# The Tanh of a split gate block written straight to its rows by ScalarE, in two of four groups, with later landings in the plan

## The chip, the cores and the metric

One NeuronCore of a Trainium2 chip runs the whole program as one launch. The metric is device time in microseconds (us), median of three runs. The core has five engines that run side by side and wait for each other through semaphores: TensorE (PE in the profile, its weight loads PEld), VectorE (DVE), ScalarE (ACT), GpSimd (POOL) and SyncE (SP), which here only issues DMA transfers. Each engine takes its instructions in the order in which they stand.

## The reference

One inference step of a two-layer trunk over 1024 prompt tokens and 8 x 4 sample tokens, 1056 columns in all, all in fp32. The first layer is a gated linear recurrence (RG-LRU). The change lies in its two gates r and i:

```python
def _rg_lru(xc, w_r, b_r, w_i, b_i, lam, h0):
    xh = xf.reshape(Bsz, T, N_BLK, BLK_W)              # 16 blocks of 96 channels
    r = sigmoid(einsum('btni,nij->btnj', xh, w_r).reshape(Bsz, T, W) + b_r)
    ig = sigmoid(einsum('btni,nij->btnj', xh, w_i).reshape(Bsz, T, W) + b_i)
    log_a = -LRU_C * softplus(-lam) * r
    a = exp(log_a)
    bterm = sqrt(-expm1(2.0 * log_a)) * (ig * xf)
    _, h = associative_scan(_lru_combine, (a, bterm), axis=1)
```

Before it stand a norm, an input projection (1024 to 2 x 1536) and a causal convolution of four taps; after it a product with silu of the gate half and an output projection with a residual. The second layer (HGRN2, a recurrence with a matrix as its state) and a last norm follow. The sigmoid is written as a Tanh of half the argument.

## The kernel before

Channels lie on partitions, tokens along the free dimension, in three chunks of 352 columns. A product in nearly full precision is three matmuls (lines 290 to 292): high part times high, high times low, low times high.

The 1536 channels of the first layer are 12 tiles of 128, in four groups g = 0 to 3 of three tiles j = 0 to 2. A group holds four blocks of 96 channels. Three of them lie whole in one tile each; the fourth is cut in three parts of 32 channels, and the part of tile j lies on partitions 32j to 32j+31 of that tile. So for each group, chunk c and gate i (0 for r, 1 for i) there are four gate products, into banks of PSUM named `hg` (four of them):

- three for the tiles j, whose Tanh (line 666) goes to `R[:, i, j]`, all 128 rows;
- a fourth for the split block (called the fo gate here). Its input is gathered first by six small DMAs from the tiles into `fo` (two parts, high and low, of three tiles; 32 rows each). Its result has 96 rows, 32 for each tile, on the very partitions that they have in the tiles. Its Tanh (line 672) goes to a buffer `td` in the tile `ST`, and three DMAs of 32 rows, `R<-ST`, copy it over the rows of `R` that the whole-tile Tanh left without meaning.

`R` has two slots, used by the chunks in turn; a slot comes free when the scans of its chunk are done. From `R` the chain goes on: exp (line 679) and a second Tanh (line 681) for each tile, a Sqrt over all three (line 689, which takes a load of another activation table ahead of it and one behind), then on VectorE the products (lines 686, 690, 692), the scan (line 706) and the product with the gate (line 716).

All this runs beside products: the input projections and convolution of the next group (lines 566 to 598) and the output projection of an earlier group (line 737 adds the residual, whose pieces SP loads and stores by DMA as `x1a` and `x1b`). SP issues nearly every DMA of the layer, the six `fo<-Z` and the three `R<-ST` of each gate among them.

The order on each engine is not written by hand. Each operation is handed to an object `Flow` with an engine, a duration, what it reads and writes; `plan` runs a list schedule over this, and the operations are emitted in the order that it found. It has a rule for when a DMA has landed, in microseconds of its own clock `t0`; `kb` is the size in kilobytes:

```python
elif kb:
    dma = max(dma, t0 + 2.6) + kb / 250.0
```

A search of 3000 random tries then improves the first 60 us of the first layer. The second layer has its own `Flow`, whose other rule for landings (`exact`) the change leaves alone. The plan only sets the order; on the chip each instruction starts when its engine and its semaphores allow.

Of the kernel before, what the change touches and what calls it, by code (L numbers as in the profile page):

```python
# [18 lines left out]
AF = mybir.ActivationFunctionType  # L19
# [31 lines left out]
CH = 352  # L51
# [9 lines left out]
class Flow:  # L61
# [67 lines left out]
    def plan(self, key, stop=None):  # L129

        n = len(self.ops)
        left = [len(o[3]) for o in self.ops]
        ready = list(self.born)
        wait = {e: [] for e in self.ENGINES}
        free = dict(self.busy)
        dma = locked = taken = 0.0
        for i in range(n):
            if not left[i]:
                wait[self.ops[i][0]].append(i)
        starts, ends, took, order = [0.0] * n, [0.0] * n, [0.0] * n, []  # L140
        for _ in range(n):
            t0, e = min((max(free[e], min(ready[i] for i in q)), e) for e, q in wait.items() if q)
            q = wait[e]
            i = min((j for j in q if ready[j] <= t0), key=lambda j: (key[j], j))
            q.remove(i)
            order.append(i)
            _, us, _, _, _, kb, _, both = self.ops[i]
            if both and not self.exact and free["POOL"] > t0:
                us = max(us, free["POOL"] - t0 + us - 0.13)
            elif both and self.exact:  # L150
                us += max(0.0, taken - t0 - 0.07)
                locked = t0 + us
            elif e == "POOL" and self.exact:
                us += max(0.0, locked - t0 - 0.035)
                taken = t0 + us
            starts[i] = t0
            free[e] = end = t0 + us
            if kb and self.exact:
                dma = max(dma + kb / 250.0, t0 + 2.4 + kb / 600.0)
                end = dma - 2.15 - kb / 250.0  # L160
            elif kb:
                dma = max(dma, t0 + 2.6) + kb / 250.0
                end = dma - 2.15 - kb / 250.0
            ends[i] = max(free[e], dma if kb else 0.0)
            took[i] = us
            if i == stop:
                break
            for j in self.after[i]:
                ready[j] = max(ready[j], free[e] if (i, j) in self.soft else end + self.lag(i, j))
                left[j] -= 1  # L170
                if not left[j]:
                    wait[self.ops[j][0]].append(j)
        last = max(t for t, o in zip(ends, self.ops) if self.until in (None, o[0]))
        return last, starts, ends, order, took
# [83 lines left out]
def tile_trunk(ctx: ExitStack, tc: tile.TileContext, xT, xN, prm, hc, w0, wg, wo0, w1, wo1, s_in,  # L258
               yT, h_out, c_out, sp_out, ss_out):
    nc = tc.nc  # L260
    V, S, G, T, Q = nc.vector, nc.scalar, nc.gpsimd, nc.tensor, nc.sync
# [12 lines left out]
    R = work.tile([128, 4, TOK], F32, tag="R", name="R")  # L274
# [13 lines left out]
    def mm3(out, w, xh, xl, first, last, more=False):  # L288
        wh, wl = w
        T.matmul(out, wh, xh, start=first, stop=False, skip_group_check=more)  # L290
        T.matmul(out, wh, xl, start=False, stop=False, skip_group_check=more)  # L291
        T.matmul(out, wl, xh, start=False, stop=last, skip_group_check=more)  # L292
# [12 lines left out]
    sm = const.tile([128, 12 * 16], F32, name="smalls")  # L305
# [39 lines left out]
    with ExitStack() as l0:  # L345
# [3 lines left out]
        def fixed(name, shape, dt=F32, pool=None):  # L349
            return (pool or pl).tile(shape, dt, tag=name, name=name)  # L350
# [7 lines left out]
        def dma(dst, src, r=(), w=(), prio=5, kb=180, q=Q, chain=None):  # L358
            fl.add("SP" if q is Q else "ACT", 0.45, lambda: q.dma_start(dst, src), r, w, prio, kb * (1.0 if r or fl.exact else 0.75),
                   line=chain)  # L360

        def act(n, emit, r, w, prio=5, more=0.0, chain=None):
            fl.add("ACT", (0.09 + 0.00088 * n if fl.exact else 0.25 + 0.0007 * n) + more, emit, r, w, prio, line=chain)
# [24 lines left out]
        t0 = fixed("t0", [128, 3, NB])  # L388
# [26 lines left out]
        def xpart(j, i, c):  # L415

            b = 6 * c + 2 * j + i
            return X[:, b * CH:(b + 1) * CH], ("X", b)
# [34 lines left out]
        def product(w, xs, step=8, more=(), bank=None):  # L453

            ps, pk = bank or next(mm)
            n = len(xs)
            for s in range(0, n, step):
                ks = range(s, min(n, s + step))

                def emit(ks=ks):  # L460
                    for k in ks:
                        mm3(ps[:, :CH], w(k)[:2], *xs[k][:2], k == 0, k == n - 1)

                fl.add("PE", (0.484 if fl.exact else 0.48) * len(ks), emit, (*(q for k in ks for q in (*xs[k][2], *w(k)[2])), *more), (pk,), 1, main=True)
            return ps, pk
# [164 lines left out]
        def lru(g):  # L630
# [16 lines left out]
            for c in range(NCH):  # L647
                s = c % 2
                R = R2[s]
# [3 lines left out]
                for j in range(3):  # L653
                    w = slice(32 * j, 32 * j + 32)
# [3 lines left out]
                for i, hb in ((0, hbr), (1, hbi)):  # L658
                    for j in range(3):
                        m = 3 * g + j  # L660
                        ps, pk = next(hg)
                        (a, ak), (b, bk) = xpart(j, 0, c), xpart(j, 1, c)
                        u = 3 * i + j
                        fl.add("PE", 0.48, lambda ps=ps, a=a, b=b, u=u: mm3(ps[:, :CH], (gh[:, u, :], gl[:, u, :]), a, b, True, True),
                               (ak, bk, ("gh", u // 4 * 4), ("gl", u // 4 * 4)), (pk,), 0)
                        act(CH, lambda ps=ps, R=R, i=i, j=j, hb=hb, m=m: S.activation(R[:, i, j], ps[:, :CH], AF.Tanh, bias=hb[:, m:m + 1],  # L666
                                                                           scale=0.5), (pk, ("sm",)), (("R", s, i, j),), 2, 0.05)
                    ps, pk = next(hg)

                    fl.add("PE", 0.48, lambda ps=ps, i=i: mm3(ps[:, :CH], (gsh[:, i, :], gsl[:, i, :]), fo[:, 0], fo[:, 1], True, True),  # L670
                           (("gs",), ("gsl",), ("fo",), *(("fo", n, j) for n in range(2) for j in range(3))), (pk,), 0)
                    act(CH, lambda ps=ps, i=i: S.activation(td[:, i], ps[:96, :CH], AF.Tanh, bias=hbd[:96, 4 * i + g:4 * i + g + 1],
                                                            scale=0.5), (pk, ("sm",)), [("ST", j, i) for j in range(3)], 2, 0.05)
                    for j in range(3):
                        w = slice(32 * j, 32 * j + 32)
                        dma(R[w, i, j], td[w, i], (("ST", j, i),), (("R", s, i, j),), 2, 45)
# [446 lines left out]
        yd = [nc.dram_tensor(f"yd_{h}", (128, TOK), F32, kind="Internal").ap() for h in range(H - 2)]  # L1123
        x1b = [nc.dram_tensor(f"x1b_{m}", (128, TOK), F32, kind="Internal").ap() for m in range(KD)]
        lru(0)
        split_y(0)
        run(project0(gate(1)))
        run(project0(conv(1)))
        gates, rest = project0(gate(2)), out(0, xT, x1a)
        run(islice(gates, 6))  # L1130
        lru(1)
        run(gates)
        run(project0(conv(2)))
        lru(2)
        run(rest)
        split_y(1)
# [19 lines left out]
    with ExitStack() as l1:  # L1156
# [644 lines left out]
        def yparts(c):  # L1801
            return [(yh[k][:, chunk(c)], yl[k][:, chunk(c)], (("yh", k, c), ("yl", k, c))) for k in range(K1)]
# [22 lines left out]
        for n, (m, c) in enumerate([(m, c) for c in range(NCH) for m in range(2)] + [(m, c) for m in range(2, KD) for c in range(NCH)]):  # L1825
# [11 lines left out]
            ps, pk = product(ws2[m], yparts(c), 8 if m > 1 else 1)  # L1837
# [90 lines left out]
        for (a, n), RM, SM in zip(OUT, RMS, SMS):  # L1928
# [4 lines left out]
            for m in range(KD):  # L1933
# [9 lines left out]
                ps, pk = next(mm)  # L1943
# [96 lines left out]
```

## Time and profile before

| what | us |
|---|---|
| median of 3 runs | 1031.67 (1030.27 to 1032.05) |
| the profiled execution | 1029.75 |
| its span in the trace | 1027.9 |
| TensorE busy | 1013.2, 99% of the span |
| VectorE, ScalarE, GpSimd busy | 777.6, 610.3, 494.6 |
| Tanh to `ST` (line 672) | 24 of 548 ns each |

The span begins with the first instruction and ends with the last; the execution's own time is 1.85 us longer. "Busy" for TensorE is modelled from start times, since matmuls overlap, so the count of matmuls that start in a stretch of fixed length tells more than its busy share. Times within the trace are us from the span's start. The first layer takes up about 0 to 510; its groups 2 and 3 have their gates between about 220 and 390. In a view of waits, a row names the waiting engine and line, what it waited for, the total, how many times, and the longest.

### The profile page before, as it was taken

To read this page: it belongs to the slowest core of one execution; us is meant where nothing else is said; L and a number is where in the kernel's file an instruction comes from. 1 tells how busy PE (TensorE), PEld (TensorE's weight loads), DVE (VectorE), ACT (ScalarE), POOL (GpSimd) and SP (SyncE) were. 2 spreads that over 40 slices of the span, in tenths; PEclk is the share of its full clock that TensorE was granted. 3 is DMA by queue.
4 is the path that set the end of the run, shared out by engine and by line. 5 is a ranking of instruction groups with operands and counts; after the bars stand their busy time and mean duration, and the time that the engine had idled before them with its cause. 6 is when DMAs were issued, how large, how long until landed. Compare 5 with 4: busy or idle time off the path is not lost.

```text
span 1027.9 us, 25651 instructions
## 1 busy us (share of the span) xinstructions
PE 1013.2 (99%) x9981; PEld 993.5 (97%) x9981; DVE 777.6 (76%) x1538; ACT 610.3 (59%) x1405; POOL 494.6 (48%) x579
## 2 busy tenths in 40 slices
PE   9999999999999999999999999999999999999997
PEld 9999999999999999999999999999999999999986
DVE  6899986798689688557798787787777777885537
ACT  7678656876765666434566474646565564752324
POOL 2435453454247254744235655564646464641544
PEclk9999999999999999999999999999999999999999
DMA  9611111214652478622113142423333333666204
GB/s 283 204 53 43 51 61 61 79 55 134 202 186 71 145 224 270 201 72 77 62 32 125 46 141 89 127 87 126 106 119 111 106 125 98 212 197 208 87 1 170
DMA packets 84442, 124.60 MB, mean 121 GB/s; under 512 B 11296, under 2 KB 61728, under 8 KB 84320
## 3 DMA queue, kind: packets, MB, share of 16 engines
q1 hardware_dynamic: 75104, 107.13, 33.6%
q10 hardware_dynamic: 9216, 15.84, 4.8%
q8 instruction: 78, 1.28, 0.5%
q14 instruction: 44, 0.36, 0.1%
HBM read 82.55 MB, written 33.87 MB: 113 GB/s over the span
## 4 chain that ended last, share of the span: by engine, by line
PE 86%; DVE 5%; ACT 3%; issue 2%; DMA 2%; POOL 1%; SPq 0%; POOLq 0%; DVEq 0%; ACTq 0%
PE mm L290 24%; PE mm L292 24%; PE mm L291 24%; PE hg L1281 2%; DVE k L594 2%; DMA R<-ST 1%; PE hg L1470 1%; PE hg L291 1%; PE hg L290 1%; PE hg L1513 1%; PE hg L292 1%; PE hg L1515 1%; PE hg L902 1%; PE hg L1538 1%; DVE R L706 1%
## 5 line engine op out<-in xcount | busy, mean ns | idle before, releaser
L290 PE MATMUL mm<-xh,whi 128*128 128x352 f32 (+1 forms) x1111 | 343.0, 309 | 0.3 <-DVE xo L737 0.3
L291 PE MATMUL mm<-xl,whi 128*128 128x352 f32 (+1 forms) x1111 | 340.8, 307 | 1.0 <-POOL xl L374 1.0
L292 PE MATMUL mm<-xh,wlo 128*128 128x352 f32 (+1 forms) x1111 | 341.5, 307 | 0.0
L374 POOL TENSOR_TENSOR wlo<-wraw,whi 128x256 fp32r<-128x256 f32 (+3 forms) x190 | 194.4, 1040 | 180.4 <-ACT whi L436 81.4
L291 PEld LDWEIGHTS mm<-xl,whi 128*128 128x128 f32 x1111 | 209.1, 188 | 1.5 <-POOL xl L374 1.2
L290 PEld LDWEIGHTS mm<-xh,whi 128*128 128x128 f32 x1111 | 208.8, 188 | 1.1 <-issue 0.6
L292 PEld LDWEIGHTS mm<-xh,wlo 128*128 128x128 f32 x1111 | 208.8, 188 | 0.2 <-DVE wlo L374 0.2
L290 PE MATMUL mm<-Z,whi 128*128 128x264 f32 (+1 forms) x507 | 152.2, 300 | 0.0
L291 PE MATMUL mm<-Z,whi 128*128 128x264 f32 (+1 forms) x507 | 150.5, 297 | 0.0
L292 PE MATMUL mm<-Z,wlo 128*128 128x264 f32 (+1 forms) x507 | 150.5, 297 | 0.0
L290 PEld LDWEIGHTS mm<-Z,whi 128*128 128x128 f32 x507 | 95.3, 188 | 2.7 <-ACT xh L1798 1.5
L594 DVE SCALAR_TENSOR_TENSOR k<-xb,prm_sb,k 128x352 f32<-128x352 f32 (+2 forms) x144 | 91.8, 646 | 7.4 <-ACT k L591 4.5
L291 PEld LDWEIGHTS mm<-Z,whi 128*128 128x128 f32 x507 | 95.5, 188 | 0.3
L292 PEld LDWEIGHTS mm<-Z,wlo 128*128 128x128 f32 x507 | 95.5, 188 | 0.2 <-POOL wlo L762 0.2
L374 POOL TENSOR_TENSOR wlo<-R,whi 128x256 fp32r<-128x256 f32 x74 | 59.4, 822 | 47.0 <-ACT whi L1640 40.6
L685 POOL TENSOR_TENSOR k<-Z 128x352 f32<-128x352 f32 x36 | 44.4, 1242 | 74.0 <-DVE R L686 64.4
L436 ACT CAST whi<-wraw 128x512 fp32r<-128x512 f32 (+2 forms) x75 | 41.2, 568 | 28.5 <-PE mm L291 11.6
L1710 DVE TENSOR_TENSOR k<-mm,k 128x264 f32<-128x264 f32 x58 | 24.5, 425 | 40.5 <-PE mm L292 33.7
L1640 ACT CAST whi<-wraw 128x512 fp32r<-128x512 f32 x61 | 37.6, 616 | 24.5 <-PE mm L291 24.4
L1707 ACT COPY k<-mm 128x264 f32<-128x264 f32 x84 | 31.7, 377 | 32.7 <-PE mm L292 29.8
L666 ACT ACTIVATE R<-hg,smalls 128x352 f32<-128x352 f32 x72 | 38.1, 550 | 14.7 <-DVE R L706 8.4
L290 PE MATMUL mm<-xh,Z 128*128 128x352 f32 x140 | 45.7, 327 | 0.0
(455 smaller groups left out, 2337.5 us busy)
## 6 DMA issues: line engine op xcount, KB each, us to landing
wraw<-in_w_dram SPq DMA_DIRECT2D x50, 256.0 KB, 3.3
wraw<-in_w_dram ACTq DMA_DIRECT2D x39, 256.0 KB, 3.2
wraw<-in_wo_dram SPq DMA_DIRECT2D x34, 192.0 KB, 2.7
R<-in_w_dram ACTq DMA_DIRECT2D x18, 256.0 KB, 2.8
si<-in_s_in_dram SPq DMA_DIRECT2D x8, 512.0 KB, 6.2
vt<-sg SPq DMA_DIRECT2D x8, 512.0 KB, 4.0
sg<-vt SPq DMA_DIRECT2D x32, 128.0 KB, 3.4
kt<-xo SPq DMA_DIRECT2D x8, 512.0 KB, 2.6
```

Of the source, the lines that this page charges most:

```text
L290: T.matmul(out, wh, xh, start=first, stop=False, skip_group_check=more)
L291: T.matmul(out, wh, xl, start=False, stop=False, skip_group_check=more)
L292: T.matmul(out, wl, xh, start=False, stop=last, skip_group_check=more)
L374: emit = lambda: e.tensor_tensor(b, x, a.bitcast(F32), op=ALU.subtract)
L436: act(m, lambda: S.copy(hi[:, :m], raw[:, :m]), rk, (hk,), prio, chain=chains[0])
L594: dve(u, lambda src=src, dst=dst, sh=sh, k=k: V.scalar_tensor_tensor(dst, sh(src, k), pc("cw", 12 * k + m), dst, op0=ALU.mult, op1=ALU.add ...
L666: act(CH, lambda ps=ps, R=R, i=i, j=j, hb=hb, m=m: S.activation(R[:, i, j], ps[:, :CH], AF.Tanh, bias=hb[:, m:m + 1], scale=0.5), (pk, ("s ...
L685: pool(CH, lambda x=x, a=a, b=b: G.tensor_tensor(x, a.bitcast(F32), b.bitcast(F32), op=ALU.add), (ak, bk), (xk,), 3)
L1281: T.matmul(ps[32 * j:32 * j + 32, n * w:n * w + w], B[:, o:o + 32], q(slice(o, o + 32)), start=True, stop=True, tile_position=(0, 32 * j))
L1640: act(512, lambda: S.copy(hi, raw), (rk,), (hk,), 2)
L1707: act(QT, lambda: S.copy(o[0], z[0]), (z[1],), (o[1],), 0)
L1710: dve(QT, lambda: V.tensor_tensor(o[0], z[0], u[0], op=ALU.add), (z[1], u[1]), (o[1],), 0)
```

## The change

In the third and fourth group (g = 2 and 3) the fo gate's Tanh no longer goes to `td` and from there by DMA. Three Tanh instructions of 32 rows and 352 columns read the bank and write `R[w, i, j]` directly, and the `continue` leaves the three DMAs out. Groups 0 and 1 keep the buffer and the DMAs. In the plan's rule for landings, a DMA that starts between 60 and 385 us of the plan's clock counts as landed 0.8 us later than before. Lines behind the new block move down by six (679 becomes 685, 681 becomes 687, 689 becomes 695).

```diff
             elif kb:
-                dma = max(dma, t0 + 2.6) + kb / 250.0
+                dma = max(dma, t0 + (3.4 if 60.0 < t0 < 385.0 else 2.6)) + kb / 250.0
                 end = dma - 2.15 - kb / 250.0
...
                     fl.add("PE", 0.48, lambda ps=ps, i=i: mm3(ps[:, :CH], (gsh[:, i, :], gsl[:, i, :]), fo[:, 0], fo[:, 1], True, True),
                            (("gs",), ("gsl",), ("fo",), *(("fo", n, j) for n in range(2) for j in range(3))), (pk,), 0)
+                    if g in (2, 3):
+                        for j in range(3):
+                            w = slice(32 * j, 32 * j + 32)
+                            act(CH, lambda ps=ps, R=R, w=w, i=i, j=j: S.activation(R[w, i, j], ps[w, :CH], AF.Tanh, bias=hbd[w, 4 * i + g:4 * i + g + 1],
+                                                                                   scale=0.5), (pk, ("sm",)), (("R", s, i, j),), 2, 0.05)
+                        continue
                     act(CH, lambda ps=ps, i=i: S.activation(td[:, i], ps[:96, :CH], AF.Tanh, bias=hbd[:96, 4 * i + g:4 * i + g + 1],
                                                             scale=0.5), (pk, ("sm",)), [("ST", j, i) for j in range(3)], 2, 0.05)
```

Both edits change the plan's input, so the order moves on every engine through the first layer. On TensorE the last row that differs lies at the norm of the last chunk of the first layer's output; from there on, the whole second layer included, its rows stand as before.

The first place is SP's queue in group 2, ahead of the gather of the last chunk's `fo` (the second batch of six of this group; `x1a` is the residual's storage, `xo`, `k` and `xb` its landing buffers, `wraw` weights). Before:

```order
L359 DMA R<-ST 32x352
L359 DMA x1a<-xb_140 128x352
L359 DMA x1a<-k 128x352
L359 DMA k<-in_xT_dram 128x352
L359 DMA R<-ST 32x352 x2
L359 DMA k<-in_xT_dram 128x352
L359 DMA x1a<-xb_138 128x352
L359 DMA R<-ST 32x352
L359 DMA xb_139<-in_xT_dram 128x352
L359 DMA wraw<-in_w_dram 128x512
L359 DMA fo<-Z 32x352 x6
```

With the change:

```order
L359 DMA x1a<-k 128x352
L359 DMA wraw<-in_w_dram 128x512
L359 DMA xo<-in_xT_dram 128x352
L359 DMA x1a<-k 128x352
L359 DMA xo<-in_xT_dram 128x352
L359 DMA wraw<-in_w_dram 128x512
L359 DMA x1a<-k 128x352
L359 DMA k<-in_xT_dram 128x352
L359 DMA fo<-Z 32x352 x6
```

The copies to `R` are gone. Between the chunk's gather and the one ahead of it stand 20 transfers before and 17 now.

The second place is ScalarE in group 3, around the exp of the second chunk. Before, with the Tanh to `ST`, the casts of weights (436), the exps (679) and the whole-tile Tanhs (666) that empty gate banks behind them:

```order
L672 ACTIVATE ST<-hg,smalls 96x352
L436 CAST whi<-wraw 128x384 x2
L666 ACTIVATE R<-hg,smalls 128x352
L672 ACTIVATE ST<-hg,smalls 96x352
L679 ACTIVATE a<-R,smalls 128x352
L681 ACTIVATE R<-R,smalls 128x352
L679 ACTIVATE a<-R,smalls 128x352
L681 ACTIVATE R<-R,smalls 128x352
L666 ACTIVATE R<-hg,smalls 128x352 x2
```

With the change (675 is the new Tanh):

```order
L675 ACTIVATE R<-hg,smalls 32x352
L666 ACTIVATE R<-hg,smalls 128x352
L675 ACTIVATE R<-hg,smalls 32x352 x2
L685 ACTIVATE a<-R,smalls 128x352
L666 ACTIVATE R<-hg,smalls 128x352
L687 ACTIVATE R<-R,smalls 128x352
L685 ACTIVATE a<-R,smalls 128x352
L666 ACTIVATE R<-hg,smalls 128x352
L675 ACTIVATE R<-hg,smalls 32x352 x3
L687 ACTIVATE R<-R,smalls 128x352
L685 ACTIVATE a<-R,smalls 128x352
L687 ACTIVATE R<-R,smalls 128x352
```

The exp now stands behind Tanhs of its own engine, and Tanhs that empty gate banks stand between the exps, where before two stood behind two exps.

## The prediction

> **What bounds the kernel now.** I read the page's busy line first, then the table of stretches, then the waits of TensorE, and from there the timelines of the engines that it waited for.
>
> ```profile
> PE 1013.2 (99%) x9981; PEld 993.5 (97%) x9981; DVE 777.6 (76%) x1538; ACT 610.3 (59%) x1405; POOL 494.6 (48%) x579
> 100.00:150.00 50.00, 50.00 (x313) 50.00 (x313) 45.34 (x80) 29.58 (x63) 23.34 (x24) 1.00 0.18 53
> 250.00:300.00 50.00, 48.23 (x296) 47.16 (x295) 39.05 (x66) 34.37 (x58) 19.50 (x19) 1.00 0.73 221
> 300.00:350.00 50.00, 49.49 (x308) 49.20 (x308) 42.16 (x72) 30.70 (x69) 25.57 (x32) 1.00 0.27 79
> 350.00:400.00 50.00, 48.13 (x292) 46.61 (x291) 35.41 (x55) 39.47 (x65) 22.07 (x16) 1.00 0.76 235
> ```
>
> TensorE sets the time; only its lost time can be won. The stretches count its matmuls: 313 in 50 us where nothing disturbs it, 0.16 us apiece. The three stretches that hold groups 2 and 3 have 17, 5 and 21 fewer: 43 matmuls, 6.9 us. The clock was granted in full (1.00), so these are waits. More than 6.9 us is not to be had from these groups. Finer stretches place the loss (64 matmuls is a full one):
>
> ```profile
> 100.00:110.00 10.00, 10.00 (x64) 10.00 (x64) 10.00 (x13) 3.88 (x10) 7.23 (x6) 1.00 0.17 58
> 270.00:280.00 10.00, 8.52 (x51) 8.04 (x51) 7.73 (x12) 6.88 (x9) 1.56 (x1) 1.00 0.70 212
> 280.00:290.00 10.00, 9.71 (x59) 9.12 (x58) 8.62 (x12) 4.20 (x8) 8.02 (x7) 1.00 0.87 259
> 330.00:340.00 10.00, 9.49 (x60) 9.20 (x59) 9.75 (x21) 5.97 (x15) 4.47 (x9) 1.00 0.22 62
> 350.00:360.00 10.00, 9.79 (x58) 8.99 (x57) 2.88 (x6) 9.56 (x14) 2.07 (x2) 1.00 0.61 179
> 360.00:370.00 10.00, 8.79 (x55) 8.44 (x53) 8.07 (x12) 5.70 (x12) 4.93 (x3) 1.00 0.77 235
> 370.00:380.00 10.00, 9.55 (x57) 9.28 (x58) 7.19 (x11) 8.37 (x13) 6.22 (x5) 1.00 0.60 171
> ```
>
> Call the loss at 270 to 280 A (13 matmuls, 2.1 us), at 280 to 290 B (5, 0.8), at 330 to 340 C (4, 0.65), at 350 to 360 D (6, 1.0), at 360 to 380 E (16, 2.6). What ended each is in TensorE's waits from 255 to 400 us:
>
> ```profile
> PE hg L290 <- ACT R L666: 1.5, 1, 1.5
> PE hg L290 <- DMA fo<-Z: 1.2, 1, 1.2
> PE hg L291 <- DVE Z L598: 0.5, 1, 0.5
> PE mm L290 <- DVE xo L737: 0.3, 1, 0.3
> ```
>
> The first is E: a gate product found no free bank, since ScalarE had not run the Tanh that empties one. The second is A: the gather of `fo` was late. C and B wait for VectorE.
>
> **Part 1: the copies leave the chain (E and D).** ScalarE's timeline shows why the bank was late:
>
> ```profile
> 350.33 0.68 ACT L679 ACTIVATE a<-R,smalls 128x352 f32<-128x352 f32 x1 [2.92 <-DMA R<-ST]
> 362.51 0.55 ACT L672 ACTIVATE ST<-hg,smalls 96x352 f32<-96x352 f32 x1
> 367.08 0.69 ACT L679 ACTIVATE a<-R,smalls 128x352 f32<-128x352 f32 x1 [4.02 <-DMA R<-ST]
> 369.68 0.98 ACT L666 ACTIVATE R<-hg,smalls 128x352 f32<-128x352 f32 x2
> ACT a L679 <- DMA R<-ST: 9.2, 5, 4.0
> ```
>
> The exp needs the 32 rows that the DMA brings. After the Tanh to `ST` ended at 363.1 ScalarE stood idle for 4.0 us, and behind the waiting exp stood the two Tanhs that empty gate banks; they ran at 369.68, and TensorE's gate product followed. D is the same with 2.9 us. The changed order has only ScalarE's own Tanhs ahead of the exp, so no landing is waited for. These two places go: 1.0 + 2.6 = 3.6 us.
>
> Here the Trainium skill speaks against the change: "DMA: Bandwidth & Descriptors", Rules for kernel authors, has a DMA issued early and its semaphore waited for late, so that the fixed cost overlaps with compute; by that rule the copies would be free and removing them worth 0. The 9.2 us in the last row disagree for this place.
>
> **Part 2: SP's queue (A).** It was full from 249 to 293 us:
>
> ```profile
> L359 SPq DMA_DIRECT2D R<-ST x13: 507/513/582, 249.8 to 292.7; - x13
> 263.57 0.51 SPq L359 DMA_DIRECT2D R<-ST  x1
> 265.76 1.15 SPq L359 DMA_DIRECT2D R<-ST  x2
> 268.11 0.51 SPq L359 DMA_DIRECT2D R<-ST  x1
> 269.82 3.68 SPq L359 DMA_DIRECT2D fo<-Z  x6
> 272.73 0.32 PE L292 MATMUL mm<-Z,wlo 128*128 128x352 f32 x1
> 274.25 0.40 PE L290 MATMUL hg<-fo,gsh 128*128 128x352 f32 x1 [1.20 <-DMA fo<-Z]
> ```
>
> The fo gate started 4.4 us after the first of the six issues (274.25 - 269.82). Ahead of them four copies took 0.51 + 1.15 + 0.51 us with about 0.05 us between issues: 2.3 us. Without them the gather starts at 267.5 and the gate could start at 271.9, ahead of the 272.9 at which TensorE got there. The wait of A goes: 2.1 us. In the order with the change 54 matmuls (8.7 us) stand between the last fo gate of the chunk before and this one, as before, and SP has 17 transfers in between in place of 20; in group 3, between the last two gathers, 14 in place of 23.
>
> **Part 3: what ScalarE pays.** Twelve Tanhs of 96 rows become 36 of 32. No row shows that form. The nearest:
>
> ```profile
> L672 ACT ACTIVATE ST<-hg,smalls 96x352 f32<-96x352 f32 x24 | 13.2, 548 | 1.0 <-PE hg L292 0.5 <-DMA R<-ST 0.3
> L666 ACT ACTIVATE R<-hg,smalls 128x352 f32<-128x352 f32 x72 | 38.1, 550 | 14.7 <-DVE R L706 8.4 <-POOL ST L711 2.4 <-PE hg L292 2.0
> L1345 ACT COPY attn<-attnd 32x256 f32<-32x256 f32 x32 | 12.9, 403 | 0.8 <-DVE attnd L1285 0.5
> L1350 ACT COPY attn<-hg 32x128 f32<-32x128 f32 x16 | 4.0, 249 | 3.0 <-PE hg L1360 2.4 <-DVE attn L1350 0.3
> ```
>
> 96 and 128 rows cost the same (548 and 550 ns), so height does not count; the copies of 32 rows grow by 154 ns for 128 columns, which puts 352 columns at 0.52 us. Bounds 0.52 and 0.55; I take 0.55, the row of the same function. The 24 added Tanhs are 13.2 us of ScalarE. Over 250 to 400 us it was busy for 34.4 + 30.7 + 39.5 = 104.6 of 150 us and waited 9.2 us for these copies, so 13.2 - 9.2 = 4.0 us come out of 36 us that it stood idle for other reasons. That hides the cost on average. Where gates stand close it may not: a bank of an fo gate comes free after 3 x 0.55 us in place of one, 1.1 us later, and each of the twelve could hold up the next gate by that. Bounds: nothing, and 4.0 us, all that ScalarE carries beyond what it no longer waits for. Only four of the twelve stand where gates came too late in the trace (D and E); I take 1.2 us, about one such delay.
>
> Best Practices in "Trainium Kernel Development and Optimization" of the Trainium skill says to tile to 128 partitions; three pieces of 32 break it, and by it this edit is a loss on ScalarE. [...]
>
> **Part 4: a new wait on ScalarE.** The Tanh to `ST` needed no slot of `R`. The new one writes `R`, so it waits until the scans of two chunks earlier are done, with every bank behind it. Whole-tile Tanhs wait so already, 4.8 us in all:
>
> ```profile
> ACT R L666 <- DVE R L706: 4.8, 2, 4.0
> ```
>
> The fo Tanhs stand in the new order behind a whole-tile Tanh of the same slot, which has had that wait by then. Bounds 0 and 4.0 us (the longest); I take 0.
>
> **Part 5: later landings, and the rest of the order.** In the stretch 245 to 392 us the DMAs of the copies' buffer landed after:
>
> ```profile
> DMA to landing us min/median/max: 1.8/3.2/5.2
> ```
>
> The plan's 2.6 + 44 KB x 4 ns was 2.8 us, now 3.6: nearer this median, so gates that need a gather are placed later. C and B (1.45 us) wait for VectorE, whose work this does not change: I leave them where they are, though the first gate of C moved nine matmuls (1.4 us) later. Groups 0 and 1 are re-planned too, with their copies kept. The stretch from 60 to 260 us shows no loss (the x313 row stands for it), so nothing can be won and something lost. The bound above is the density of groups 2 and 3, 6.9 us in 150, over these 200 us: 9.2 us. That density came from copies and gathers that were later than planned, and the new plan has them later, so I take 0.2 us, near the zero of the row itself.
>
> **The sum**, against the profiled execution (1029.75 us, of which 1027.9 us span): A 2.1 + D 1.0 + E 2.6 = 5.7 us less; 1.2 + 0.2 = 1.4 us more; net 4.3 us less, 1025.45. The median of the runs shown is 1.9 us above that execution, so for a median: 1031.67 - 4.3 = **1027.4 us**. Behind the first layer TensorE's order is unchanged, and what is won there arrives at the end.
>
> **Rivals.** *The time moves to other waits.* With the copies gone the chain's next late link is VectorE: exps done sooner meet scans still queued behind the convolution, and the next gates wait for slots of `R` as they waited for copies. For it: VectorE was 97% busy from 330 to 340. Against it: in D and E VectorE had time (2.88 of 10 us at 350 to 360). Then only A is won, 2.1 us, and the 1.4 us are paid: 1031.0.
>
> *ScalarE becomes the bound (slower).* From 350 to 360 it was busy for 9.56 of 10 us while TensorE lost time. If the gates keep standing where ScalarE is that full, every fo gate holds the next one up by its 1.1 us: 12 x 1.1 = 13.2 us against 5.7 won, 1039.2. An fo gate pays once ScalarE has less than 1.1 us to spare between it and the gate that takes its bank next; from the sixth that pays (5.7 / 1.1 = 5.2) the change is a loss. Against it: 36 us of idle in the three stretches.
>
> *The new plan costs more in groups 0 and 1 than it wins.* Three new waits of the size of A (2.1 us) would turn the gain into 2.0 us of loss: 1033.7. For it: VectorE is busier there (45.34 of 50 us in the x313 row) than later. Against it: the row of zero loss, under a plan that counted on earlier landings. *The edit does nothing that the plan would not do*: the gates moved by the landings alone avoid A and E, and the direct Tanh adds only its cost; the time would be the forecast's, and only a run with one edit tells.
>
> **Numbers.** A difference under 0.2%, 2.1 us, cannot be told from none here. Forecast 0.66 (4.3 us; from all of 6.9 us down to 2.5), other waits 0.18 (1031.0), ScalarE or groups 0 and 1 slower 0.12, between them 0.04. Faster: 0.66 and a third of the second, 0.72. Slower 0.10, the rest 0.18 the same. The range runs from 1031.67 - 6.9 = 1024.8 to 1032.0, past the second case; the forecast's own is 1024.8 to 1029.2.
>
> **What would show it.** Right: from 250 to 300 and 350 to 400 us the count of matmuls is at least 305 each; no row in which ScalarE or VectorE waits for `R<-ST` after 250 us; the new Tanhs at 0.52 to 0.56 us; ScalarE's busy time up by 13 us; SP with idle time ahead of the gathers. Wrong: TensorE's waits name Tanh lines 666 or 675 with 3 us or more, or waits appear between 60 and 250 us; or the Tanh of 32 rows costs well over 0.55 us.

## The result, and the profile after

| | before | after |
|---|---|---|
| median of 4 runs, us | 1030.97 (1030.16 to 1032.05) | 1024.81 (1023.94 to 1025.56) |
| the profiled execution, us | 1029.75 | 1025.03 |
| its span, us | 1027.9 | 1023.3 |

The ratio is 0.9939, with a 95% interval from 0.9922 to 0.9957: 6.2 us less, 4.4 to 8.0. A second comparison on another chip gave 0.9952 [0.9940, 0.9965], 4.9 us. The pair of profiled executions differs by 4.7 us. So the change makes the kernel faster, as forecast. The first comparison has 6.2 us where the sum had 4.3, with a median at the fast end of the forecast's own range (1024.8); the second has 4.9 us (3.6 to 6.2).

The page's busy line of the changed kernel:

```profile
PE 1012.5 (99%) x9981; PEld 994.0 (97%) x9981; DVE 782.6 (76%) x1538; ACT 623.6 (61%) x1429; POOL 494.2 (48%) x579
```

ScalarE is busy 13.3 us longer (623.6 - 610.3), nearly the 13.2 us of part 3, and TensorE is still 99% busy. The three stretches of groups 2 and 3, with the columns as in the prediction:

```profile
250.00:300.00 50.00, 48.77 (x303) 48.53 (x302) 41.02 (x73) 45.74 (x77) 18.88 (x20) 1.00 0.71 226
300.00:350.00 50.00, 50.00 (x313) 50.00 (x312) 42.44 (x71) 31.48 (x71) 24.52 (x32) 1.00 0.27 84
350.00:400.00 50.00, 50.00 (x311) 49.77 (x310) 39.31 (x61) 47.15 (x82) 23.59 (x19) 1.00 0.79 243
```

303, 313 and 311 matmuls stand where 296, 308 and 292 stood: 12 are missing from three times 313 in place of 43. At 0.16 us each that is 1.9 us lost in place of 6.9, a gain of 5.0 us. ScalarE's columns went from 34.4, 30.7 and 39.5 us to 45.7, 31.5 and 47.2: two of the three stretches are nearly full now.

Where E stood, ScalarE's timeline now reads:

```profile
363.45 1.12 ACT L675 ACTIVATE R<-hg,smalls 32x352 f32<-32x352 f32 x2
364.60 0.68 ACT L685 ACTIVATE a<-R,smalls 128x352 f32<-128x352 f32 x1
365.31 0.55 ACT L666 ACTIVATE R<-hg,smalls 128x352 f32<-128x352 f32 x1
365.76 0.67 ACT L687 ACTIVATE R<-R,smalls 128x352 f32<-128x352 f32 x1
366.33 0.67 ACT L685 ACTIVATE a<-R,smalls 128x352 f32<-128x352 f32 x1
```

Line 685 is the exp (679 before). It starts when the direct Tanh ends, with no wait, and the Tanh 666 that empties a bank follows at once. What TensorE still waits for between 200 and 420 us is one row:

```profile
PE hg L290 <- ACT R L666: 1.2, 1, 1.2
```

This wait did not exist before. It lies at 250 us, in the first gates of group 2, and the timeline shows its history:

```profile
248.65 0.49 ACT L597 CAST Z<-k 128x352 fp32r<-128x352 f32 x1 [2.86 <-DVE k L594]
249.04 0.51 ACT L436 CAST whi<-wraw 128x384 fp32r<-128x384 f32 x1
249.57 1.28 ACT L666 ACT_TABLE_LOAD   x1
250.87 0.55 ACT L666 ACTIVATE R<-hg,smalls 128x352 f32<-128x352 f32 x1
251.47 0.43 PE L290 MATMUL hg<-Z,gh 128*128 128x352 f32 x1 [1.23 <-ACT R L666]
```

ScalarE waited 2.86 us for VectorE's convolution (line 594) before a cast. A cast of weights and a load of the table (1.28 us) stood between that cast and the Tanh that empties the first bank. No direct Tanh has run by then; the first one starts at 254.3. The lost time here, taken from the starts of the matmuls around it, is 1.5 us.

### The profile page after: what moved, and what is told of

It reads as the page before. It is cut to its first block, busy times and chain, and to the rows that moved or that the text cites. A ratio compares the mean times of both kernels' runs of the same rounds, so it can differ in the third digit from the quotient of the medians.

```text
span 1023.3 us, 25600 instructions
## 1 busy us (share of the span) xinstructions
PE 1012.5 (99%) x9981; PEld 994.0 (97%) x9981; DVE 782.6 (76%) x1538; ACT 623.6 (61%) x1429; POOL 494.2 (48%) x579
## 3 DMA queue, kind: packets, MB, share of 16 engines
q8 instruction: 78, 1.28, 0.5%
## 4 chain that ended last, share of the span: by engine, by line
PE 93%; DVE 2%; ACT 1%; DMA 1%; POOL 1%; issue 1%; SPq 0%; POOLq 0%; DVEq 0%; ACTq 0%
PE mm L290 26%; PE mm L292 26%; PE mm L291 26%; PE hg L1287 2%; PE hg L290 2%; PE hg L291 2%; PE hg L292 2%; PE hg L1476 1%; PE hg L1519 1%; PE hg L1521 1%; DMA sg<-in_xN_dram 1%; PE hg L1544 1%; PE hg L1374 0%; DMA sg<-in_xT_dram 0%; POOL sg L1919 0%
## 5 line engine op out<-in xcount | busy, mean ns | idle before, releaser
L374 POOL TENSOR_TENSOR wlo<-wraw,whi 128x256 fp32r<-128x256 f32 (+3 forms) x190 | 191.4, 1024 | 184.5 <-ACT whi L436 90.9
L594 DVE SCALAR_TENSOR_TENSOR k<-xb,prm_sb,k 128x352 f32<-128x352 f32 (+2 forms) x144 | 89.7, 633 | 10.7 <-ACT k L591 5.5
L290 PE MATMUL mm<-xh,Z 128*128 128x352 f32 x140 | 45.8, 327 | 0.0
L292 PE MATMUL mm<-xh,Z 128*128 128x352 f32 x140 | 45.2, 323 | 0.0
```

What stands on the lines that cost most here:

```text
L374: emit = lambda: e.tensor_tensor(b, x, a.bitcast(F32), op=ALU.subtract)
L594: dve(u, lambda src=src, dst=dst, sh=sh, k=k: V.scalar_tensor_tensor(dst, sh(src, k), pc("cw", 12 * k + m), dst, op0=ALU.mult, op1=ALU.add ...
```

## The experiments

Eleven runs of ten kernels were made, each of five executions or more, beside the kernel before on the same chip. The last two columns are what the trace says: matmuls started in 250 to 300, 300 to 350 and 350 to 400 us, and how many of 3 x 313 are missing, times 0.16 us.

| kernel | median, us | ratio to before, interval | matmuls | lost, us |
|---|---|---|---|---|
| before, four sets | 1029.9 to 1031.2 | | 296, 308, 292 | 6.9 |
| changed, again | 1025.00 | 0.9952 [0.9940, 0.9965] | 305, 313, 313 | 1.3 |
| direct Tanh alone | 1023.18 | 0.9926 [0.9913, 0.9939] | 313, 312, 313 | 0.2 |
| the same, again | 1023.46 | 0.9933 [0.9920, 0.9945] | 313, 313, 312 | 0.2 |
| later landings alone | 1030.93 | 0.9997 [0.9985, 1.0009] | 306, 313, 286 | 5.4 |
| copies in the new order | 1051.49 | 1.0198 [1.0182, 1.0215] | 254, 288, 268 | 20.6 |
| idle copies added | 1028.22 | 0.9973 [0.9964, 0.9982] | 297, 313, 298 | 5.0 |
| each direct Tanh twice | 1033.97 | 1.0039 [1.0027, 1.0052] | 291, 295, 286 | 10.7 |
| one of three twice | 1026.51 | 0.9958 [0.9945, 0.9971] | 305, 311, 304 | 3.0 |
| direct in group 2 only | 1027.09 | 0.9960 [0.9945, 0.9975] | 313, 313, 276 | 5.9 |
| direct in group 3 only | 1026.18 | 0.9955 [0.9943, 0.9967] | 297, 313, 313 | 2.6 |
| direct in all groups | 1024.10 | 0.9944 [0.9930, 0.9957] | 312, 313, 313 | 0.2 |

6.9 less the last column follows the measured gain (by the ratio) to 1.2 us in all rows but two (the copies in the new order, and group 2 only), of which the text says more.

### Which edit does it

The theory was that the direct Tanh brings the gain, by its two effects: no landing ahead of the exp, no copies in SP's queue. The rival was that the later landings in the plan would do the same by moving the gates. Each edit was made alone. The direct Tanh alone:

```diff
-                dma = max(dma, t0 + (3.4 if 60.0 < t0 < 385.0 else 2.6)) + kb / 250.0
+                dma = max(dma, t0 + 2.6) + kb / 250.0
```

> The direct Tanh in groups 2 and 3 alone, the plan's landings left at 2.6 us. The order on TensorE then stands as before up to the gates of group 2 (about 245 us). Theory (copies on ScalarE's chain and in SP's queue cost the time): the waits A, D and E are gone without any help of the later landings, TensorE makes at least 305 matmuls in 250 to 300 and in 350 to 400 us, and the time is 5 to 7 us below before, 1024 to 1026. Rival (the later landings moved the gates out of the way): the time stays within 2 us of before, 1029 to 1033.

Measured: 1023.18 us, by the ratio 7.6 us under the kernel before. Its stretches lose nothing:

```profile
250.00:300.00 50.00, 50.00 (x313) 50.00 (x312) 39.25 (x69) 44.84 (x75) 17.20 (x17) 1.00 0.69 211
300.00:350.00 50.00, 50.00 (x312) 50.00 (x312) 41.48 (x69) 33.37 (x75) 25.22 (x33) 1.00 0.36 105
350.00:400.00 50.00, 50.00 (x313) 50.00 (x312) 39.51 (x57) 45.65 (x79) 26.39 (x20) 1.00 0.72 223
```

The later landings alone:

```diff
-                    if g in (2, 3):
+                    if False:
```

> The later landings alone, with the Tanh to the buffer and the copies kept in all groups. Theory: the copies still take SP's queue and still hold up the exp, so ScalarE keeps waiting for them by more than 4 us in all after 250 us; the time is within 2.5 us of before, 1028.5 to 1033. Rival: the plan now reckons with the copies, waits A, D and E go, and the time is 1024 to 1026.

Measured: 1030.93 us, by the ratio 0.3 us under the kernel before, which cannot be told from none. The exp waits for the copies again, as the waits of ScalarE and TensorE from 250 to 420 us show:

```profile
ACT a L685 <- DMA R<-ST: 7.9, 5, 3.7
PE hg L290 <- ACT a L685: 1.7, 1, 1.7
PE hg L290 <- ACT R L666: 0.8, 1, 0.8
```

The table of stretches shows that the rival holds for one part: with the landings alone the losses A, B and C shrink (306 and 313 matmuls in the first two stretches in place of 296 and 308), while the third loses more (286 in place of 292). A later landing in the plan moves a gate behind its gather; it does not take the exp out of the chain. The gain of the change is therefore the direct Tanh's.

The direct Tanh alone was 1.6 us better than the whole change, on different chips. Both were run again on one chip.

> The changed kernel once more, beside the direct Tanh without the later landings, on one chip. If the later landings cost nothing, both give the same time, between 1023 and 1025 us. If they cost the new wait of ScalarE and TensorE at 250 us (1.5 us) and the 1.2 us more at the start, this one is 1.5 to 2.7 us above the other.

> Direct Tanh in groups 2 and 3, the plan's landings left at 2.6. If the first run's 1.6 us below the change was the chip and not the kernel, it falls within 0.5 us of the changed kernel here. If it was the order, it is again 1.5 us or more below, with no lost matmul between 60 and 420 us.

Measured: 1025.00 and 1023.46 us, 1.5 us apart as in the first runs. The wait at 250 us stands in both traces of the change (1.5 and 1.2 us lost) and in that of the landings alone (1.0 us), and in neither trace of the direct Tanh alone. So the landings cost about what this wait costs, and the direct Tanh alone is the best version that was found. The first 60 us, the other half of what was expected here, do not separate the two: 357 and 353 matmuls start there in the two traces of the change, 357 and 352 in the two of the direct Tanh alone (362 in the trace of the kernel before). They vary from execution to execution.

### Does each loss have its place, or is it a lucky order

A new plan moves hundreds of instructions. If the gain came from that alone, it would not be bound to a group. The direct Tanh was made in one group at a time, with the landings of the kernel before.

```diff
-                    if g in (2, 3):
+                    if g == 2:
```

> Direct Tanh in group 2 alone, landings left at 2.6. By parts 1 and 2 each loss has its place: the copies in SP's queue at 263 to 268 us (A) are those of group 2, the exps that wait (D, E) stand in group 3. Then A goes (2.1 us, with B 2.9) and D and E stay (3.6): 1.8 to 2.9 us under the kernel before, with waits of exp for R<-ST and lost matmuls only after 340 us. Rival that the direct Tanh only gives the plan another order, which happens to be good: no place is bound to a group, and either all is won (6 us) or nothing.

```diff
-                    if g in (2, 3):
+                    if g == 3:
```

> Direct Tanh in group 3 alone, landings left at 2.6. By the same parts: D and E go (3.6 us, with C 4.2), A and B stay (2.9): 3.6 to 4.2 us under the kernel before, lost matmuls between 260 and 300 us and none from 340 to 400. Rival of the lucky order: as above, all or nothing, or losses in other places.

Measured: 1027.09 us for group 2 alone (4.1 us less, 2.6 to 5.7) and 1026.18 for group 3 alone (4.6 us less, 3.4 to 5.9). The places are those that were named. With group 2 alone, the stretch that holds A and B is whole and the loss is in group 3:

```profile
270.00:280.00 10.00, 10.00 (x64) 10.00 (x63) 8.39 (x15) 8.58 (x13) 4.86 (x4) 1.00 0.76 251
280.00:290.00 10.00, 10.00 (x64) 10.00 (x63) 10.00 (x13) 7.28 (x13) 5.78 (x5) 1.00 0.93 300
350.00:400.00 50.00, 47.51 (x276) 47.01 (x276) 34.77 (x58) 37.56 (x64) 21.54 (x16) 0.93 0.75 233
```

With group 3 alone it is the other way round:

```profile
270.00:280.00 10.00, 9.38 (x56) 8.56 (x54) 7.23 (x12) 8.74 (x12) 1.85 (x2) 1.00 0.68 205
280.00:290.00 10.00, 10.00 (x61) 9.51 (x60) 9.52 (x12) 3.18 (x8) 9.29 (x7) 1.00 0.93 289
350.00:400.00 50.00, 50.00 (x313) 50.00 (x312) 39.87 (x64) 45.64 (x79) 23.59 (x19) 1.00 0.81 252
```

The rival of the lucky order falls as the main cause. Both medians are somewhat past what was expected (2.9 and 4.2 us at most), with the expected ends inside the intervals. C (0.65 us), counted only in the second, is gone in both; so much a new order does by itself. With group 2 alone, the gain in the table (6.9 - 5.9 = 1.0 us) falls short of the measured 4.1: the profiled execution was the longest of six, 1029.0 us of 1024.68 to 1029.0, and what happened in it at 366 us is told in the last section. The loss there is in the place that was named, but not by the wait that was named: TensorE waited for a gather (1.8 us), not for a bank. Ahead of that gather SP issued three copies in one piece (1.78 us from 360.08), so it is part 2's mechanism in group 3.

### What the copies cost by themselves: the chain, and the queue

To have the queue's share alone, an idle transfer was added behind each direct Tanh, at its place in SP's queue and with the copy's shape. Its data goes to a scratch array that nobody reads; the order is otherwise that of the change.

```diff
+                            def piece(ps=ps, R=R, w=w, i=i, j=j, c=c):
+                                S.activation(R[w, i, j], ps[w, :CH], AF.Tanh, bias=hbd[w, 4 * i + g:4 * i + g + 1], scale=0.5)
+                                Q.dma_start(nc.dram_tensor(f"dum_{g}_{c}_{i}_{j}", (32, CH), F32, kind="Internal").ap(), td[w, i])
```

> The changed kernel and its order, with 36 transfers of 32 x 352 from the unused buffer to memory that nobody reads, issued on SP where the direct Tanhs stand. Nobody waits for them; they only take SP's queue as the copies did. Theory by its second part: the gathers of fo are late again by up to 2 us at one to three places, 1 to 4 us more than the changed kernel, 1026 to 1029. Rival (SP's queue was never the point, only the exp's wait was): within 1 us of the changed kernel, 1024 to 1026.

Measured: 1028.22 us, 3.4 and 3.2 us above the two medians of the change (by the centres of the ratios 3.5 and 2.2); the lost time in the three stretches rises from 1.9 to 5.0 us. Three places of lost time are new. At 377 us a gather is late again, as SP's timeline in group 3 shows:

```profile
371.14 1.15 SPq L359 DMA_DIRECT2D fo<-Z  x2
372.34 0.57 SPq L678 DMA_DIRECT2D dum<-ST  x1
372.95 0.51 SPq L359 DMA_DIRECT2D fo<-Z  x1
...
375.30 1.14 SPq L359 DMA_DIRECT2D fo<-Z  x2
377.41 0.40 PE L290 MATMUL hg<-fo,gsh 128*128 128x352 f32 x1 [0.82 <-DMA fo<-Z]
```

In the changed kernel the same six stood in one piece, and their gate product waited for nothing:

```profile
369.37 3.70 SPq L359 DMA_DIRECT2D fo<-Z  x6
374.93 0.32 PE L290 MATMUL hg<-fo,gsh 128*128 128x352 f32 x1
```

The issue of the last of the six ended at 373.1 there and at 376.4 here: three idle transfers stand between the six and hold SP for 0.58 us each. At 357 us TensorE waited 0.6 us for VectorE's addition to the residual, which had itself waited 2.8 us for the piece that SP loads. The third place, a fo gate at 285.9 us, is put down to a cast on ScalarE (0.6 us). So 36 transfers that nobody waits for cost 3.4 us. Part 2's mechanism is shown by the gather at 377 us. How much of the rest is SP's time and how much the added traffic was not separated, and the size is that of these 36 places, not of A, where the copies of the kernel before stood elsewhere.

The other experiment put the copies back in full, at the direct Tanhs' places in the new order: one Tanh of 96 rows to `td` in place of the first of three, and a copy in place of each.

```diff
-                            act(CH, lambda ...: S.activation(R[w, i, j], ps[w, :CH], AF.Tanh, ...), (pk, ("sm",)), (("R", s, i, j),), 2, 0.05)
+                            def piece(ps=ps, R=R, w=w, i=i, j=j, seen=seen):
+                                if not seen:
+                                    seen.append(1)
+                                    S.activation(td[:, i], ps[:96, :CH], AF.Tanh, bias=hbd[:96, 4 * i + g:4 * i + g + 1], scale=0.5)
+                                Q.dma_start(R[w, i, j], td[w, i])
...
+                            act(CH, piece, (pk, ("sm",)), (("R", s, i, j),), 2, 0.05)
```

> The changed kernel's order on all engines, but in groups 2 and 3 the first of each three Tanhs writes 96 rows to the buffer, and the copies are issued on SP where the three Tanhs stood. Theory: waits for R<-ST are back on ScalarE (more than 5 us) and the gates behind them stall TensorE; 1029 to 1036. Rival (the order is what pays): 1024 to 1027, as the changed kernel.

Measured: 1051.49 us, 20 us above the kernel before, and far above what was expected. The waits of ScalarE and TensorE name it:

```profile
ACT a L692 <- DMA R<-ST: 40.2, 12, 7.4
PE hg L290 <- ACT R L666: 8.0, 6, 2.6
PE mm L290 <- ACT whi L436: 3.1, 1, 3.1
```

The exp waited twelve times, 40.2 us in all, where before it waited five times, 9.2. The loss goes on past the three stretches: from 400 to 450 us 266 matmuls started, 47 or 7.5 us fewer, so 28 us are lost in all, 21 more than before. This order was planned with the rows of `R` ready when ScalarE's own Tanh ends, so it puts the exp right behind. It says nothing on what the copies cost in the order that was planned for them; it says that the direct Tanh and the order found for it belong together, and that what stands behind a waiting exp on ScalarE (bank Tanhs, casts of weights) reaches TensorE in this order.

The Trainium skill, "DMA: Bandwidth & Descriptors", Rules for kernel authors, has a DMA that is issued early and waited for late overlap its fixed cost with compute. The runs agree for groups 0 and 1, which keep their copies while TensorE loses nothing from 60 to 249 us. Here they do not: the copies cost TensorE time both through the exp and, with nobody waiting for them, through the queue.

### What ScalarE still has to spare

Part 3 charged the 24 added Tanhs 1.2 us, and one rival let every fo gate pay 1.1. Both were tried by adding more of the same, in the order of the change. Every direct Tanh twice:

```diff
+                            def piece(ps=ps, R=R, w=w, i=i, j=j):
+                                for _ in range(2):
+                                    S.activation(R[w, i, j], ps[w, :CH], AF.Tanh, bias=hbd[w, 4 * i + g:4 * i + g + 1], scale=0.5)
```

> The changed kernel in its own order, each of the 36 direct Tanhs issued twice on the same rows: 36 x 0.55 = 19.8 us more of ScalarE, the result the same. The Tanhs stand in 250 to 300 and 350 to 400 us, 18 in each, 9.9 us more in each; ScalarE had 4.3 and 2.8 us idle there. Theory that idle time covers them on average (the backlog is worked off where TensorE does not wait for it): the time of the change, at most 2 us above. Rival that ScalarE is at its bound in these two stretches: 5.6 + 7.1 = 12.7 us above the change, about 1037, with TensorE waiting for lines 666 and 675. I expect a part of the second, 1028 to 1035.

Measured: 1033.97 us, 9.0 us above the change on the same chip and 4.0 above the kernel before. ScalarE is full in two of the stretches (47.66 and 48.32 of 50 us), and TensorE's waits from 240 to 420 us, behind them, name it:

```profile
250.00:300.00 50.00, 47.57 (x291) 46.42 (x290) 35.88 (x63) 47.66 (x83) 18.80 (x20) 1.00 0.73 225
350.00:400.00 50.00, 48.05 (x286) 45.58 (x285) 33.60 (x55) 48.32 (x81) 18.80 (x17) 1.00 0.72 222
```

```profile
PE hg L290 <- ACT R L666: 3.1, 4, 1.4
PE hg L290 <- ACT Z L597: 1.6, 1, 1.6
PE hg L290 <- ACT R L678: 0.8, 2, 0.4
```

(Line 678 is the direct Tanh of this kernel.) Then only the last of the three pieces twice:

```diff
-                                for _ in range(2):
+                                for _ in range(2 if j == 2 else 1):
```

> The changed kernel in its own order, the last of the three direct Tanhs of each fo gate issued twice: 12 x 0.55 = 6.6 us more of ScalarE, 3.3 in each of the two stretches that have 4.3 and 2.8 us idle. If idle time covers what ScalarE pays until it is full, this costs 0 to 1 us: 1025 to 1026. If every added Tanh costs the same from the first on, as 36 of them cost 9.0 us, it costs 12 x 0.25 = 3.0 us: 1028.

Measured: 1026.51 us, 1.5 us above the change by the medians, 0.6 to 2.0 by the centres of the ratios. That is between the two expectations. The trace has new lost time of 1.1 us at 347 to 352 and 0.8 at 363, in addition to the wait at 250. Together the runs give a curve: the 24 Tanhs that the change adds cost TensorE nothing that any trace shows (the direct Tanh alone loses nothing in its three stretches), 12 more cost about 1.5 us (0.13 each), and the 24 after these another 7.5 (0.31 each). One rival is left: the plan knew of the first 24 and not of the others, which stand in an order made without them. So the runs show that this order has no room for more; that an order planned for 12 more would have none either is not shown.

### Would more of the same help

```diff
-                    if g in (2, 3):
+                    if True:
```

with the landings of the kernel before.

> Direct Tanh in all four groups, landings at 2.6. TensorE lost nothing from 60 to 250 us with the copies of groups 0 and 1 in place, so by the theory that only lost TensorE time can be won there is nothing to gain: 1023 us, as with groups 2 and 3 alone. Rival that the copies cost something in every group: another 3 to 6 us less, under 1020. Rival that ScalarE's further 13.2 us fall where it is full (35 of 50 us busy before): up to some 3 us more, with TensorE waiting for a Tanh before 250 us.

Measured: 1024.10 us, against 1023.46 for groups 2 and 3 alone on the same chip: no further gain. Its three stretches are whole (312, 313, 313), as are those of the version beside it. Where TensorE lost nothing (60 to 250 us), taking copies away wins nothing.

## Where the prediction was right, and which step failed

**What bounds the kernel**: right. The lost matmuls of TensorE, at 0.16 us each, follow the time through the runs, from 0.2 us lost at 1023 us to 10.7 at 1034.

**Part 1 (D and E)**: right. No row of the changed kernel has ScalarE or VectorE waiting for `R<-ST` after 250 us. With the direct Tanh in group 3 alone the stretch 350 to 400 is whole; with the landings alone, or in group 2 alone, it is not. But a wait of the exp does not always reach TensorE: with the direct Tanh in group 3 alone the exps still waited five times for copies, 6.6 us in all, and TensorE waited for none of ScalarE's Tanhs. VectorE's wait for the copies was the larger one, as its waits in the kernel before from 250 to 420 us show:

```profile
DVE R L686 <- DMA R<-ST: 15.1, 7, 3.9
```

In the changed kernel the same product (line 692) waits 2.9 us for the direct Tanh in its place.

**Part 2 (A)**: right in mechanism. The idle copies bring a late gather back. The sign "SP with idle time ahead of the gathers" was too much: for 3.7 us ahead of the second gather of group 2 SP still issues almost back to back, and the pause before that is a wait of SP's own (1.6 us, for GpSimd). What the gather gained is the distance to its gate, 8.5 us from the first issue in place of 4.4, and the gate waits for nothing:

```profile
276.90 3.68 SPq L359 DMA_DIRECT2D fo<-Z  x6
285.44 0.32 PE L290 MATMUL hg<-fo,gsh 128*128 128x352 f32 x1
```

**Part 3**: the price was right, the charge was not. The page's row of the new form:

```profile
L675 ACT ACTIVATE R<-hg,smalls 32x352 f32<-32x352 f32 x36 | 19.6, 544 | 1.0 <-PE hg L292 0.4
```

544 ns for 32 rows against 548 for 96 and 550 for 128: height does not count, as was taken. "Best Practices" in "Trainium Kernel Development and Optimization" of the Trainium skill says to tile to 128 partitions. By this row three short pieces do cost three full prices, and the time came down nevertheless. The 1.2 us charged to TensorE were not paid: the direct Tanh alone loses nothing. **Part 4** (no new wait for a slot of `R`): right; the 1.0 us of idle ahead of line 675 names no scan. (The 4.8 us "in all" of its row are those between 255 and 400 us; the row of line 666 in part 3 has 14.7 us for the whole program.)

**Part 5** failed in both its terms. It left C and B, 1.45 us, where they were, because VectorE's work does not change: they are gone. B goes wherever A goes (change, landings alone, group 2 alone) and shrinks from 5 missing matmuls to 3 where A stays (group 3 alone), with no wait of TensorE left there. Whether B followed from A or moved with the plan, no run separates. C is in none of the plans made with either edit. A wait for an engine whose work does not change still moves with the plan. The other term, 0.2 us for what the new plan loses from 60 to 260 us, was to be 1.5: the re-plan with later landings put a cast that waits 2.9 us for VectorE, a cast of weights and a table load ahead of the first gate's Tanh at 250 us, at the seam of group 1 and group 2.

**The sum.** Won in the three stretches were A to E, 6.9 us in place of 5.7; paid were 1.9 (in the trace of the second run of the change 1.3) in place of 1.4. That is 5.0 us against the 4.3 forecast. Outside of them five fewer matmuls start in the first 60 us (357 in place of 362, 0.8 us lost); the pair of profiled executions differs by 4.7 us, so 0.5 us more are won in other places. For the profiled execution the forecast was 1025.45 us and the result 1025.03. That it came so close is in part luck: the terms of parts 3 and 5 were each off by more than 1 us, and partly cancel.

**The step to the median** is the one that failed by most. The prediction added the 1.9 us by which the median of before, 1031.67, lay above the profiled execution, as if this distance belonged to the program. In the changed kernel the median lies 0.2 us below its profiled execution (1024.81 and 1025.03), in the second run of the same kernel 0.7 above (1025.00 and 1024.29). So the distance is the spread of single executions and does not carry over; it makes 2.1 of the 2.6 us between the forecast of 1027.4 and the measured median, and the other 0.4 is the profiled execution's. The second comparison, 4.9 us, is nearer to the forecast's 4.3 than the first.

Why executions of one kernel differ stays open. Those of the kernel before range from 1028.96 to 1035.17 us in one set of 21, those of the change from 1023.94 to 1025.84 in nine, and only one execution of each set has a trace. The granted clock bears on it: of 41 executions of the kernel before, run beside the experiments, the 22 with a mean clock of 0.998 or more average 1030.1 us, the 19 with less 1031.7. No trace of a long execution of that kernel shows where its clock fell.

**The signs.** No wait of ScalarE or VectorE for `R<-ST`, the price of the Tanh and ScalarE's 13 us came as said. The count of at least 305 matmuls was missed in the first stretch (303; 305 in the second run) by the wait at 250 us, which also lies at the edge of the sign of being wrong, "waits appear between 60 and 250 us".

**The rivals.** *Other waits*: one appeared (250 us), of 1.5 us. TensorE waited for ScalarE there, which had waited for VectorE as the rival has it, but for the convolution and not for a slot of `R`. *ScalarE becomes the bound*: it did not, but 36 Tanhs more in the same order come to 4.0 us above the kernel before. *Groups 0 and 1*: no wait of TensorE between 60 and 249 us in either trace of the change. *The plan alone would do it*: A, B and C yes, the time no (0.9997).

## What to carry to other kernels

A copy by DMA that only moves rows to where an engine could have written them itself is paid in two places that its own length does not show: whatever stands behind its reader in that engine's queue, and whatever stands behind it in the queue that issues it. Three short instructions at full price each can be cheaper than one and three copies, as long as the engine has idle time in that very stretch, to be read there and not from the page's average. The distance between a profiled execution and a median is no term of a forecast until several executions show that it is constant. And when an edit changes a planner's input, run each part of the edit alone: here one part brought all of the gain and the other took 1.5 us of it back.

## What was not expected of the hardware

After some waits of TensorE the granted clock fell to half for a few microseconds, once at a price as large as the wait. With the direct Tanh in group 2 alone, the gather was late at 366 us. TensorE's timeline, and behind it two finer stretches of the same kernel:

```profile
366.44 0.32 PE L292 MATMUL hg<-Z,gl 128*128 128x352 f32 x1
368.55 0.43 PE L290 MATMUL hg<-fo,gsh 128*128 128x352 f32 x1 [1.79 <-DMA fo<-Z]
369.67 0.63 PE L291 MATMUL hg<-fo,gsh 128*128 128x352 f32 x1 [0.69 <-issue]
370.11 0.49 PE L292 MATMUL hg<-fo,gsl 128*128 128x352 f32 x1
370.40 0.50 PE L290 MATMUL hg<-Z,gh 128*128 128x352 f32 x1
```

```profile
366.00:370.00 4.00, 1.51 (x7) 1.01 (x6) 1.64 (x3) 3.94 (x6) 0.00 (x0) 0.86 0.32 85
370.00:375.60 5.60, 5.60 (x20) 5.60 (x20) 3.57 (x6) 3.50 (x6) 3.53 (x4) 0.50 0.73 197
```

From 370.1 on, 19 matmuls started 0.29 us apart in place of 0.16, with the clock at 0.50: 19 x 0.13 = 2.5 us lost with TensorE waiting for nothing, behind two gaps of 2.1 and 1.1 us between starts. This would account for the 1.9 us by which this execution lies above its kernel's median. The landings alone and the copies in the new order each have such stretches of 11 matmuls, behind gaps of 2.0 to 3.4 us between two starts. It does not follow each time, and not by the length of the gap alone. In the copies in the new order a gap of 2.9 us at 259 us has no such stretch behind it. The first 30 us of the direct Tanh in all groups and of the second run of the direct Tanh alone have the same wait at 21.3 and 21.1 us (1.67 and 1.59 us between starts), and only the first fell to half clock, as the stretch from 20 to 30 us shows, first of all groups:

```profile
20.00:30.00 10.00, 8.65 (x45) 8.14 (x44) 5.53 (x16) 4.24 (x9) 4.42 (x5) 0.83 0.85 243
```

and of groups 2 and 3 alone:

```profile
20.00:30.00 10.00, 8.73 (x55) 8.22 (x54) 7.05 (x19) 5.29 (x11) 4.25 (x6) 1.00 0.78 226
```

The Trainium skill, "TensorE: Matmul & The Clock Gate", Part 1, has a free-running window of about 3.4 us that sets the clock to half after an idle window, so that the same program differs from run to run. The stretches of 11 matmuls (3.2 us) and the differing pair agree with it. The gaps do not: 1.67, 2.0 and 2.5 us were enough, each less than the whole idle window that the Trainium skill asks for.
